# Modulation weights of a diffusion layer: 32 blocks over eight groups of tokens, all dot products on VectorE

## The chip, the cores and the metric

The kernel runs on one core of a Trainium2 chip. The metric is the device time of one execution, in microseconds. Five engines work beside each other, each with its own queue that is carried out in order: TensorE (PE; its weight loads are listed as PEld), VectorE (DVE), ScalarE (ACT), GpSimd (POOL) and SyncE (SP), which here issues all DMA transfers. Engines wait for each other by semaphores.

## The reference

One layer of a diffusion model in float32: 2048 latent tokens and 128 context tokens, width 1024. The part at issue comes first:

```python
def modulation(cond, w_ada, b_ada):
    m = jax.nn.silu(cond) @ w_ada + b_ada
    return jnp.split(m, 6, axis=-1)      # shift, scale, gate for attention and for the FFN

sa, ca, ga, sf, cf, gf = modulation(...)          # once for c, once for c_ctx
u = rms_norm(x, g_pre) * (1.0 + scale) + shift
p = u @ w_in                                       # q, k, v, B, C, x_in
```

`w_ada` is 1024 by 6144. It is used with two conditioning vectors, one for the latent and one for the context tokens. Then come differential attention (q and k of the latent tokens are rotated, softmax over 2176 keys), a gated short convolution, the output projection, and a SwiGLU FFN. Shift and scale of the attention (2048 columns) are needed before the first projection. The other 4096 columns (shift and scale of the FFN, both gates) are needed only after attention.

## The kernel before, in words

`w_ada` is stored transposed, in 48 blocks of 128 output columns (on partitions) by 1024 inputs, 512 KB each. For a block and a condition vector `ada_sum` makes 128 dot products of length 1024. On DVE (V) that is one instruction, line 139, which multiplies `raw` by the condition `cb` and sums into a column of `mc` (the full products go to `jv` and are not used). On POOL (G) it is a product, line 143 (`prod`), and a sum on ACT, line 144. The first 16 blocks are handled by `ada_first` before and during the first group of tokens; they are as they were.

Blocks 16 to 47 are handled by `ada_later`: one load (`raw`, four buffers), the dot product with the first vector on DVE, and that with the second on POOL for two blocks of three and on DVE for the third, as the string `LATER` says. So 32 + 11 products are on DVE and 21 on POOL. Small DVE instructions then turn the columns into `modc` (lines 149 to 151) or `gates` (line 174).

Phase 1 makes q, k and v in nine groups of tokens: eight of 256 latent tokens and one of the 128 context tokens, in the order 0, 1, 2, 8, 3, 4, 5, 6, 7 (8 is the context). Per group, `qkv_group` goes through k, q, v: 24 matmuls for each 128 tokens (lines 238 to 240, accumulator `pq`, four buffers). DVE reads `pq` for the rotation (line 291 and twice line 297, tile `t`), POOL adds the two parts (line 299), ACT and DVE split the sum into a high and a low part (`st`; lines 82 and 83), PE transposes it (line 250), ACT or DVE copies it out (`sto`, lines 254 and 256), and it is stored. Beside it, the next group is prepared: its rows are loaded (`xt`), scaled by POOL (line 203), transposed by PE (line 222, `up`), scaled and shifted by DVE (line 224, `ut`) and split (`uh`, `ul`).

After k, q and v of each group a step (`rows_step`, then `part_step` twice) prepares the next group and takes the next `PER` = 2 blocks from `ada_work`. So blocks 16 to 47 fall on the first six groups of the order: six to a group, two to the sixth. After the seventh (n == 6) the pools of the blocks and of the condition vectors are closed, and their room goes to phase 2.

The order on each engine is not the program's order: a scheduler with a model of the engines sets it when the kernel is built. Each instruction takes its place by when the model has it ready, so a product can stand before or after the group in which it is written. SP's queue has the loads of blocks, rows and weights, and all stores, in one order.

Phase 2 (attention, the convolution and the projection), the FFN and the end follow.

Of the kernel before, what the change touches and what calls it, by code (L numbers as in the profile page):

```python
# [32 lines left out]

POOLW = 960
WLV = (2,)
LATER = "GGV"
RAWS, PER, FIRST = 6, 2, "VG"
RATE = (670, 1500)


# [1 line left out]
def layer(ctx, tc, x_prompt, x_sample, cache_k, cache_v, cond, w_ada, b_ada, gcol,  # L42
# [3 lines left out]
    V, S, G, T = nc.vector, nc.scalar, nc.gpsimd, nc.tensor  # L46
# [24 lines left out]
    def dma(out, in_):  # L71

        out, in_ = (x.bitcast(F32) if x.dtype == F32R else x for x in (out, in_))
        with tc.issue_after(behind[0]) if behind else ExitStack():
            return nc.sync.dma_start(out, in_).ins
# [54 lines left out]
    def ada_load(b):  # L130
        raw = ad.tile([P, D], F32, tag="raw", name="raw", bufs=RAWS if b < 16 else 4)
        first[b] = dma(raw, w_ada[b])
        return raw

    def ada_sum(b, raw, c, eng):

        if eng is V:
            junk = cbp.tile([P, D], BF16, tag="jv", name="jv")
            V.scalar_tensor_tensor(junk, raw, 1.0, cb[:, c, :], op0=ALU.mult, op1=ALU.mult,
                                   accum_out=mc[:, b, c:c + 1])  # L140
        else:
            prod = cbp.tile([P, D], F32, tag="prod", name="prod", bufs=1)
            G.tensor_tensor(prod, raw, cb[:, c, :], op=ALU.mult)
            S.activation(prod, prod, AF.Copy, accum_out=mc[:, b, c:c + 1])

    def ada_cols(i, kt, cs):

        b = 8 * i + 2 * kt
        V.tensor_scalar(modc[:, i + 1, cs, kt], mc[:, b, cs], bc[:, b:b + 1], None, op0=ALU.add)
        V.tensor_scalar(modc[:, i, cs, kt], mc[:, b + 1, cs], bc[:, b + 1:b + 2], 1.0, op0=ALU.add, op1=ALU.add)  # L150
        V.tensor_scalar(modc[:, i, cs, kt], modc[:, i, cs, kt], gc[:, i // 2, kt:kt + 1], None, op0=ALU.mult)
# [13 lines left out]
    def ada_later(b):  # L165
        raw = ada_load(b)
        ada_sum(b, raw, 0, V)
        ada_sum(b, raw, 1, V if LATER[b % len(LATER)] == "V" else G)
        if b < 32:
            if b % 2:  # L170
                ada_cols(2, (b - 16) // 2, slice(0, 2))
            return
        which, k = divmod(b - 32, KT)
        V.tensor_scalar(gates[:, which, :, k], mc[:, b, :], bc[:, b:b + 1], gc[:, 2 + which, k:k + 1],
                        op0=ALU.add, op1=ALU.mult)
        if b == 47:
            ps = psu.tile([P, 512], F32, tag="psu", name="gt")
            T.transpose(ps[:32, :P], gates.rearrange("p w c k -> p (w c k)"), ident)
            gt = p1.tile([32, P], F32, name="gt")
            S.copy(gt, ps[:32, :P])  # L180
            dma(ggd.rearrange("w (k n) -> (w k) n", n=P), gt)
# [24 lines left out]
    def group_rows(gi):  # L206
        if gi == 8:
            return [norm_rows(x_prompt)]
        return [norm_rows(x_sample[(2 * gi + i) * P:(2 * gi + i + 1) * P, :]) for i in range(2)]

    def u_part(xs, gi, kk, between=None):

        n, c = len(xs), int(gi == 8)
        w = n * P
        up = psu.tile([P, 512], F32, tag="psu", name="up")
        ut = p1.tile([P, 2, 256], F32, tag="ut", name="ut", bufs=2)
        h = p1.tile([P, 2, 256], F32R, tag="uh", name="uh", bufs=6)
        l = p1.tile([P, 2, 256], F32R, tag="ul", name="ul", bufs=6)
        for a in range(2):
            kt = 2 * kk + a  # L220
            for i in range(n):
                T.transpose(up[:, a * 256 + i * P:a * 256 + (i + 1) * P],
                            xs[i][:, kt * P:(kt + 1) * P], ident)
            V.tensor_scalar(ut[:, a, :w], up[:, a * 256:a * 256 + w],
                            modc[:, 0, c, kt:kt + 1], modc[:, 1, c, kt:kt + 1],
                            op0=ALU.mult, op1=ALU.add)
            if between:
                split(h[:, a, :w], l[:, a, :w], ut[:, a, :w])
                between(kt, h[:, a, :], l[:, a, :])
        if not between:  # L230
            split(h[:, :, :w], l[:, :, :w], ut[:, :, :w])
        dma(ud[gi][0, :, 2 * kk:2 * kk + 2, :w], h[:, :, :w])
        dma(ud[gi][1, :, 2 * kk:2 * kk + 2, :w], l[:, :, :w])
        return [(h[:, a, :], l[:, a, :]) for a in range(2)]
# [127 lines left out]
    def qkv_group(gi, mid):  # L362

        n = 1 if gi == 8 else 2
        rt = None
        if gi < 8:
            rt = p1.tile([P, 2, 2, 64], F32, tag="rt", name="rt", bufs=2)
            dma(rt, rope[gi])
        for j in (1, 0, 2):
            sts = []  # L370
            for i in range(n):
                if gi == 0 and j < 2:
                    pq = pq0[i, j]
                else:
                    pq = psq.tile([P, 512], F32, tag="psq", name="pq")
                    for kt in range(KT):
                        qkv_mm(pq, u[gi], i, j, kt)
                qkv_out(pq, gi, i, j, rt, sts)
            mid[j]()
            out_stack(gi, j, sts)  # L380
            if j == 1 and "k" in mid:
                mid["k"]()

    def cached():
        ck = p1b.tile([P, 512], F32, tag="t1", name="ck", bufs=2)
        dma(ck, cache_k)
        stack([heads_split(ck)], k_store(NLAT), 0)
        cv = p1b.tile([P, 512], F32, tag="t1", name="cv", bufs=2)
        dma(cv, cache_v)
        v_split(cv, 16)  # L390
# [46 lines left out]
    ada_work = list(range(16, 48))  # L437
    rows = {}
    for n, gi in enumerate(order):
        nxt = order[n + 1] if n < 8 else None  # L440

        def rows_step():
            if nxt is not None:
                rows[nxt] = group_rows(nxt)
            for b in ada_work[:PER]:
                ada_later(b)
            del ada_work[:PER]

        def part_step(a):
            if nxt is not None:  # L450
                u.setdefault(nxt, [])
                for kk in (0, 1) if a == 0 else (2, 3):
                    u[nxt] += u_part(rows[nxt], nxt, kk)
            for b in ada_work[:PER]:
                ada_later(b)
            del ada_work[:PER]

        steps = {1: rows_step, 0: lambda: part_step(0), 2: lambda: part_step(1)}
        if nxt is None:
            steps["k"] = heads_begin  # L460
        qkv_group(gi, steps)
        behind.clear()
        if n == 0:
            cached()
        if n == 6:
            x_ad.close()
            x_cb.close()
    for x in (x_psq, x_psk, x_psu, x_pb, x_p1, x_wq):
# [211 lines left out]
    def t4(name):  # L680
        return prow.tile([P, D], F32, tag="t4", name=name, bufs=4)
# [385 lines left out]
    for gn, (c, g) in enumerate(groups):  # L1067
# [3 lines left out]
        for f in range(NF):  # L1071
            raw = t4("rawo")
# [85 lines left out]
```

## Time and profile before

| | us |
|---|---|
| median of three runs | 3112.84 |
| lowest, highest | 3108.48, 3118.28 |
| the profiled execution | 3102.96 |
| its span, from the first to the last instruction | 3101.2 |
| first score product of phase 2 (line 502) | 432.7 |

Times in the profile are counted from the span's start. Phase 1 is the first 430 us of it, a seventh. A busy share there is no measure of the whole span, so stretches of phase 1 are shown by themselves. Names in the rows are those of the program's tiles, without buffer numbers. An instruction's time includes what it waits once it has started; "idle before" is the time its engine had nothing to do just before it.

### The profile page before, as it was taken

Reading aid. Unit: us, or ns where it says so; the run is one execution under the profiler, and the core shown is the slowest. Engines: PE = TensorE matmul, PEld = TensorE weight load, DVE = VectorE, ACT = ScalarE, POOL = GpSimd, SP = SyncE. Lnnn points to the kernel's source line nnn. Section 1 sums busy time; section 2 is a strip of 40 time slices with the busy share of each in tenths; the row PEclk is TensorE's granted clock in tenths of the full one; section 3 lists DMA queues with packets and bytes.
Section 4 is the critical chain, followed back from the end, with each engine's and each line's share of the span. In section 5 each row is a group of like instructions: output and inputs, shape, how many; then the busy total and the mean of one; then the engine's idle time right before and its main releaser. Section 6 shows DMA issues by size and latency. Waiting matters only on the chain.

```text
span 3101.2 us, 47350 instructions
## 1 busy us (share of the span) xinstructions
PE 2926.7 (94%) x16921; PEld 2661.2 (86%) x16921; DVE 2080.6 (67%) x4116; ACT 1370.9 (44%) x2425; POOL 1296.4 (42%) x1135
## 2 busy tenths in 40 slices
PE   4789989999999999999999999999999999999998
PEld 3567879999999999988888888999899998788886
DVE  7996547887887887764467775676655554554443
ACT  3433225665655665663444343333333333443333
POOL 7653115554554554542246554554544540111110
PEclk8899999999999999999999999999999999999999
DMA  6776473463464354347635565434643235666663
GB/s 248 234 227 218 154 244 112 120 213 107 120 191 125 109 177 129 110 152 228 203 129 161 154 192 192 155 129 147 216 156 101 96 103 187 237 227 217 219 217 121
DMA packets 351180, 525.26 MB, mean 169 GB/s; under 512 B 33088, under 2 KB 264672, under 8 KB 349152
## 3 DMA queue, kind: packets, MB, share of 16 engines
q1 hardware_dynamic: 350944, 522.23, 52.7%
q8 instruction: 133, 2.18, 0.3%
q14 instruction: 103, 0.84, 0.1%
HBM read 393.79 MB, written 128.34 MB: 168 GB/s over the span
## 4 chain that ended last, share of the span: by engine, by line
PE 65%; DVE 14%; DMA 8%; issue 7%; POOL 4%; ACT 2%; SPq 0%; POOLq 0%; DVEq 0%; ACTq 0%
PE psg L956 7%; PE psg L959 6%; PE psg L957 6%; PE s L502 6%; PE psy L1087 4%; PE psy L1085 4%; PE psy L1086 4%; PE t L546 3%; DVE wi L83 2%; DMA raw<-in_w_fi 2%; PE psx L725 2%; PE psx L726 2%; PE psx L724 2%; PE o L539 2%; DMA u2d<-hl 2%
## 5 line engine op out<-in xcount | busy, mean ns | idle before, releaser
L956 PE MATMUL psg<-u,wi 128*128 128x384 f32 (+1 forms) x1848 | 617.4, 335 | 42.6 <-ACT wi L82 18.0
L957 PE MATMUL psg<-u,wi 128*128 128x384 f32 (+1 forms) x1848 | 607.3, 329 | 0.0
L959 PE MATMUL psg<-u,wi 128*128 128x384 f32 (+1 forms) x1848 | 591.5, 331 | 4.5 <-DVE wi L83 4.5
L505 DVE TENSOR_SCALAR_CACHE_REDUCE e<-s 128x436 f32<-128x436 f32 (+2 forms) x648 | 373.4, 600 | 87.0 <-PE s L502 71.4
L956 PEld LDWEIGHTS psg<-u,wi 128*128 128x128 f32 x1848 | 351.6, 190 | 61.7 <-ACT wi L82 27.6
L959 PEld LDWEIGHTS psg<-u,wi 128*128 128x128 f32 x1848 | 348.5, 190 | 9.0 <-DVE wi L83 8.5
L502 PE MATMUL s<-km,qt 128*128 128x436 f32 (+1 forms) x1280 | 344.4, 372 | 10.8 <-DVE e L505 8.5
L957 PEld LDWEIGHTS psg<-u,wi 128*128 128x128 f32 x1848 | 352.0, 190 | 0.1
L83 DVE TENSOR_TENSOR wo<-rawo,wo 128x1024 fp32r<-128x1024 f32 x132 | 167.0, 1265 | 248.6 <-ACT wo L82 243.9
L83 DVE TENSOR_TENSOR wi<-st,wi 128x512 fp32r<-128x512 f32 x264 | 234.4, 892 | 131.3 <-ACT wi L82 129.7
L510 ACT ACTIVATE e<-e,nm 128x2176 f32<-128x2176 f32 (+1 forms) x136 | 273.9, 2014 | 76.9 <-DVE nm L509 76.2
L82 ACT CAST wi<-st 128x512 fp32r<-128x512 f32 x264 | 163.0, 620 | 324.1 <-POOL st L918 161.4
L1087 PE MATMUL psy<-wo,hhl 128*128 128x512 f32 x748 | 285.5, 390 | 1.8 <-DVE hhl L83 1.8
L1086 PE MATMUL psy<-wo,hhl 128*128 128x512 f32 x748 | 285.9, 390 | 0.9 <-DVE wo L83 0.9
L1085 PE MATMUL psy<-wo,hhl 128*128 128x512 f32 x748 | 285.6, 390 | 0.0
L82 ACT CAST wo<-rawo 128x1024 fp32r<-128x1024 f32 x132 | 139.1, 1054 | 297.7 <-PE psy L1087 288.6
L502 PEld LDWEIGHTS s<-km,qt 128*128 128x128 f32 x1280 | 209.4, 190 | 23.6 <-DVE e L505 16.3
L83 DVE TENSOR_TENSOR atl<-t,ath 128x512 fp32r<-128x512 f32 (+2 forms) x292 | 187.2, 650 | 34.2 <-ACT ath L82 33.6
L82 ACT CAST ath<-t 128x512 fp32r<-128x512 f32 (+2 forms) x292 | 157.3, 555 | 113.6 <-PE t L546 111.1
L1058 POOL TENSOR_TENSOR rr<-rr,mhalf 128x1 f32<-128x1 f32 x17 | 13.1, 779 | 450.2 <-DVE rr L1057 450.2
L918 POOL TENSOR_TENSOR st<-raw,st 128x512 f32<-128x512 f32 x66 | 103.4, 1566 | 229.7 <-DVE wi L83 229.7
L238 PE MATMUL pq<-wh,uh 128*128 128x512 f32 x408 | 172.4, 433 | 19.9 <-DVE t L297 15.2
(264 smaller groups left out, 7183.9 us busy)
## 6 DMA issues: line engine op xcount, KB each, us to landing
raw<-in_w_fi SPq DMA_DIRECT2D x132, 512.0 KB, 4.1
rawo<-in_w_fo SPq DMA_DIRECT2D x132, 512.0 KB, 3.5
fu<-ud SPq DMA_DIRECT2D x256, 256.0 KB, 4.7
raw<-in_w_ada SPq DMA_DIRECT2D x48, 512.0 KB, 4.8
u2d<-hl SPq DMA_DIRECT2D x42, 512.0 KB, 3.8
u<-u2d SPq DMA_DIRECT2D x14, 1536.0 KB, 9.5
hr<-hid SPq DMA_DIRECT2D x110, 192.0 KB, 3.5
hid<-hid SPq DMA_DIRECT2D x88, 192.0 KB, 1.9
```

The lines of the kernel that those rows point to most:

```text
L82: S.copy(h, src)
L83: (eng or V).tensor_tensor(l, src, h.bitcast(F32), op=ALU.subtract)
L238: T.matmul(pq, u[kt][0][:, sl], wh[j, kt], start=(kt == 0), stop=False)
L502: mm = T.matmul(ps[:, :n], qt[:, s, m, t * P:(t + 1) * P], km[m][:, k0:k0 + n], start=(s == 0), stop=(s == 1))
L505: V.tensor_scalar(et[:, k0:k0 + n], ps[:, :n], SCALE, None, op0=ALU.mult, op1=ALU.max, accum_out=mx[:, ci:ci + 1])
L510: S.activation(et[:, :nk], et[:, :nk], AF.Exp, bias=nm, scale=1.0, accum_out=sm[:, t, m:m + 1])
L956: T.matmul(ps[:, :n], h[:, ks], u[:, 0, kt, :n], start=start and kt == 0, stop=False, skip_group_check=not start)
L957: T.matmul(ps[:, :n], h[:, ks], u[:, 1, kt, :n], start=False, stop=False, skip_group_check=not start)
L959: T.matmul(ps[:, :n], l[:, ks], u[:, 0, kt, :n], start=False, stop=stop and kt == 3, skip_group_check=not start)
L1085: T.matmul(banks[i][:, b, :], hh, woh_[:, bs], start=(f == 0), stop=False)
L1086: T.matmul(banks[i][:, b, :], hh, wol_[:, bs], start=False, stop=False)
L1087: T.matmul(banks[i][:, b, :], hl, woh_[:, bs], start=False, stop=(f == NF - 1))
```

## The change: what it does

All second dot products of blocks 16 to 47 are on DVE as well: 64 on DVE and none on POOL. Per group of the order, four blocks are taken (two in `rows_step`, one in each `part_step`) instead of six, so the 32 blocks fall on eight groups. The pools are closed one group later. `ada_first` still puts one product of each pair on POOL.

```diff
-LATER = "GGV"
-RAWS, PER, FIRST = 6, 2, "VG"
+RAWS, FIRST = 6, "VG"
...
     def ada_later(b):
         raw = ada_load(b)
         ada_sum(b, raw, 0, V)
-        ada_sum(b, raw, 1, V if LATER[b % len(LATER)] == "V" else G)
+        ada_sum(b, raw, 1, V)
...
+        def ada_steps(k):
+            for b in ada_work[:k]:
+                ada_later(b)
+            del ada_work[:k]
+
         def rows_step():
             if nxt is not None:
                 rows[nxt] = group_rows(nxt)
-            for b in ada_work[:PER]:
-                ada_later(b)
-            del ada_work[:PER]
+            ada_steps(2)
...
-            for b in ada_work[:PER]:
-                ada_later(b)
-            del ada_work[:PER]
+            ada_steps(1)
...
-        if n == 6:
+        if n == 7:
             x_ad.close()
             x_cb.close()
```

By the order, the sequences of all engines are the same up to early in group 0's outputs and from phase 2 on; between them instructions change places. On DVE, 67 dot products become 88. Between the first of the 32 rotations (line 291) and the thirteenth, that of group 3's first 128 tokens, 43 products and 16 `gates` stood; now 47 and 7 do. Line numbers of the new kernel are lower by one in this part.

DVE before, around the first rotation of group 3 (`jv` is a dot product, `t_2011<-pq` the rotation's first part, `bl` a weight split for phase 2):

```order
L139 SCALAR_TENSOR_TENSOR jv,mc<-raw,cb 128x1024
L256 CAST sto<-tp 128x2x128
L83 TENSOR_TENSOR ul<-ut,uh 128x512
L224 TENSOR_SCALAR ut<-up,modc 128x256
L174 TENSOR_SCALAR gates<-mc,bc,gc 128x2
L91 TENSOR_SCALAR rr<-ss 128x1
L224 TENSOR_SCALAR ut<-up,modc 128x256
L91 TENSOR_SCALAR rr<-ss 128x1
L256 CAST sto<-tp 128x2x128
L83 TENSOR_TENSOR bl<-braw,bh 128x512
L291 TENSOR_TENSOR t_2011<-pq,rt 128x512
L297 TENSOR_TENSOR t_2012<-pq,rt 128x16x16 x2
```

The same place now (`t_1939` is the same rotation):

```order
L173 TENSOR_SCALAR gates<-mc,bc,gc 128x2
L138 SCALAR_TENSOR_TENSOR jv,mc<-raw,cb 128x1024 x2
L173 TENSOR_SCALAR gates<-mc,bc,gc 128x2
L138 SCALAR_TENSOR_TENSOR jv,mc<-raw,cb 128x1024
L290 TENSOR_TENSOR t_1939<-pq,rt 128x512
L296 TENSOR_TENSOR t_1940<-pq,rt 128x16x16 x2
L90 TENSOR_SCALAR rr<-ss 128x1
L290 TENSOR_TENSOR t_1973<-pq,rt 128x512
L138 SCALAR_TENSOR_TENSOR jv,mc<-raw,cb 128x1024
L223 TENSOR_SCALAR ut<-up,modc 128x256 x2
L296 TENSOR_TENSOR t_1974<-pq,rt 128x16x16 x2
L173 TENSOR_SCALAR gates<-mc,bc,gc 128x2
```

Before, the last product stood ahead of that rotation, and phase 2's weight splits had begun; now products stand right ahead of it and between the two parts of the next rotation, and go on through groups 3 and 4.

POOL before, from group 2 to group 8's rows (`t` is the rotation's sum, `prod` a product, `rr` and `xt` belong to the next group's rows):

```order
L299 TENSOR_TENSOR t_1379<-t_1379,t_1380 128x512
L143 TENSOR_TENSOR prod<-raw,cb 128x1024 x2
L299 TENSOR_TENSOR t_1413<-t_1413,t_1414 128x512
L143 TENSOR_TENSOR prod<-raw,cb 128x1024
L299 TENSOR_TENSOR t_1504<-t_1504,t_1505 128x512
L143 TENSOR_TENSOR prod<-raw,cb 128x1024 x2
L299 TENSOR_TENSOR t_1538<-t_1538,t_1539 128x512
L143 TENSOR_TENSOR prod<-raw,cb 128x1024 x2
L92 TENSOR_TENSOR rr<-rr,mhalf 128x1
L203 TENSOR_SCALAR xt<-xt,rr 128x1024
```

The same place now:

```order
L298 TENSOR_TENSOR t_1341<-t_1341,t_1342 128x512
L298 TENSOR_TENSOR t_1375<-t_1375,t_1376 128x512
L298 TENSOR_TENSOR t_1465<-t_1465,t_1466 128x512
L298 TENSOR_TENSOR t_1499<-t_1499,t_1500 128x512
L91 TENSOR_TENSOR rr<-rr,mhalf 128x1
L202 TENSOR_SCALAR xt<-xt,rr 128x1024
```

The products are gone, and the rotation's sums and the rows' instructions follow each other.

## Rows read from the trace of the kernel before

**Rows 1.** The page: the span, and each engine's busy time over it.

```profile
span 3101.2 us, 47350 instructions
PE 2926.7 (94%) x16921; PEld 2661.2 (86%) x16921; DVE 2080.6 (67%) x4116; ACT 1370.9 (44%) x2425; POOL 1296.4 (42%) x1135
```

**Rows 2.** Stretches: busy us and instructions by engine, granted clock, DMA share, GB/s.

```profile
core 0: us, PE busy (x) PEld busy (x) DVE busy (x) ACT busy (x) POOL busy (x), PEclk, DMA share, GB/s
107.00:245.00 138.00, 112.23 (x502) 87.24 (x501) 137.89 (x213) 49.60 (x92) 88.09 (x39) 0.90 0.72 234
...
290.00:410.00 120.00, 120.00 (x601) 98.05 (x600) 58.54 (x110) 27.85 (x51) 24.87 (x21) 1.00 0.53 171
```

**Rows 3.** Waits of PE, 107 to 245 us: us in total, times, longest.

```profile
PE pq L238 <- DVE t L297: 15.2, 5, 7.0
PE tp L250 <- ACT sto L254: 4.7, 2, 3.7
PE tp L250 <- DVE sto L256: 4.3, 4, 2.6
```

**Rows 4.** Waits of PE, 245 to 410 us.

```profile
PE pq L238 <- ACT uh L82: 0.4, 1, 0.4
```

**Rows 5.** DVE's groups by shape, 107 to 262 us: busy us, mean ns, idle before.

```profile
L139 DVE SCALAR_TENSOR_TENSOR jv<-raw,cb 128x1024 bf16<-128x1024 f32 x43 | 64.7, 1504 | 0.0
L151 DVE TENSOR_SCALAR modc<-modc,gc 128x2 f32<-128x2 f32 x8 | 11.1, 1388 | 0.0
L83 DVE TENSOR_TENSOR st<-t,st 128x512 fp32r<-128x512 f32 x11 | 10.4, 952 | 0.0
L149 DVE TENSOR_SCALAR modc<-mc,bc 128x2 f32<-128x2 f32 x8 | 9.0, 1123 | 0.0
L297 DVE TENSOR_TENSOR t<-pq,rt 128x256 f32<-128x256 f32 x22 | 8.2, 411 | 0.0
...
L83 DVE TENSOR_TENSOR ul<-ut,uh 128x512 fp32r<-128x512 f32 x7 | 7.4, 1058 | 0.0
...
L83 DVE TENSOR_TENSOR ul<-ut,uh 128x256 fp32r<-128x256 f32 x4 | 5.4, 1366 | 0.0
L150 DVE TENSOR_SCALAR modc<-mc,bc 128x2 f32<-128x2 f32 x8 | 4.1, 510 | 0.0
```

**Rows 6.** All dot products on DVE: ns min/median/max, first and last start.

```profile
L139 DVE SCALAR_TENSOR_TENSOR jv<-raw,cb x67: 1208/1215/3411, 8.0 to 251.8; 128x1024 bf16<-128x1024 f32 x67
```

**Rows 7.** One of the small instructions on `modc`, likewise.

```profile
L151 DVE TENSOR_SCALAR modc<-modc,gc x24: 195/209/2355, 10.9 to 191.2; 128x1 f32<-128x1 f32 x16, 128x2 f32<-128x2 f32 x8
```

**Rows 8.** DVE in order of time, 147 to 154 us: start, us, instruction.

```profile
149.83 3.41 DVE L139 SCALAR_TENSOR_TENSOR jv<-raw,cb 128x1024 bf16<-128x1024 f32 x1
```

**Rows 9.** POOL in order of time, the same stretch.

```profile
149.26 2.89 POOL L143 TENSOR_TENSOR prod<-raw,cb 128x1024 f32<-128x1024 f32 x1
```

**Rows 10.** POOL's groups by shape, 107 to 262 us.

```profile
L143 POOL TENSOR_TENSOR prod<-raw,cb 128x1024 f32<-128x1024 f32 x21 | 58.2, 2771 | 37.2 <-DMA raw<-in_w_ada 30.7 <-ACT prod L144 5.3 <-DMA qd<-sto 1.3
L299 POOL TENSOR_TENSOR t<-t,t 128x512 f32<-128x512 f32 x12 | 22.4, 1867 | 9.6 <-DVE t L297 9.6
```

**Rows 11.** DVE's groups by shape, 290 to 410 us.

```profile
L83 DVE TENSOR_TENSOR st<-t,st 128x512 fp32r<-128x512 f32 x12 | 10.0, 837 | 3.7 <-ACT st L82 3.7
...
L83 DVE TENSOR_TENSOR ul<-ut,uh 128x512 fp32r<-128x512 f32 x12 | 7.8, 688 | 1.5 <-ACT uh L82 1.4
```

**Rows 12.** DVE in order of time, 133 to 139 us.

```profile
135.41 1.21 DVE L139 SCALAR_TENSOR_TENSOR jv<-raw,cb 128x1024 bf16<-128x1024 f32 x1
...
136.55 0.22 DVE L149 TENSOR_SCALAR modc<-mc,bc 128x2 f32<-128x2 f32 x1
```

**Rows 13.** The stretch of groups 3 and 4, columns as in rows 2.

```profile
260.00:335.00 75.00, 74.64 (x378) 60.83 (x377) 41.12 (x81) 23.37 (x43) 20.16 (x15) 1.00 0.62 200
```

**Rows 14.** POOL's rotation sums: ns min/median/max, first and last start.

```profile
L299 POOL TENSOR_TENSOR t<-t,t x32: 1264/1601/3422, 100.4 to 419.1; 128x512 f32<-128x512 f32 x32
```

**Rows 15.** Phase 2's score products, likewise.

```profile
L502 PE MATMUL s<-km,qt x1280: 352/361/732, 432.7 to 1354.1; 128*128 128x436 f32 x147, 128*128 128x432 f32 x36
```

## The prediction

> **What bounds the kernel now.** I first read the page's totals [rows 1]: over the whole span TensorE (PE) is the busy engine, and VectorE (DVE) has a third of the time free. That average hides the stage the change touches, so next came the table by stretches [rows 2]. From 107 to 245 us DVE is busy for 137.89 of 138 us, PE runs 502 instructions, and its granted clock averages 0.90. From 290 to 410 us, where the same group code runs without modulation blocks, DVE is busy 58.54 of 120 us, PE runs 601 instructions without a gap, and its granted clock is 1.00. At that later rate, 120 / 601 = 0.200 us per instruction, the 502 instructions need 100.2 us. The stretch therefore loses 137.9 - 100.2 = 37.7 us, partly in gaps and partly in matmuls at the lower of the two levels (1.2 and 2.4 GHz) behind each gap. That is the most this change can return there.
>
> Third, PE's waits. The three longest kinds in that stretch are on DVE's rotation, on ACT's copy and on DVE's copy, 15.2 + 4.7 + 4.3 = 24.2 us [rows 3]; from 245 to 410 us one wait of 0.4 us is left [rows 4]. So PE is the bound after 245 us, and DVE's in-order queue is the bound before it.
>
> Fourth, why DVE is full. The groups of one shape [rows 5] show means far over what the same shapes take undisturbed. A dot product has a mean of 1504 ns against a median of 1215 [rows 6]; the three small instructions on the `modc` columns have means of 1388, 1123 and 510 ns, where the shortest takes 195 [rows 7]; `st` takes 952 and the large `ul` 1058, against some 680 of `ul` in the quiet stretch [rows 11]. The rotation's halves, which read PSUM, take 411 ns here too; the small `ul` of the same 256 columns takes 1366. One product shows the cause: it starts at 149.83 and lasts 3.41 us, and a GpSimd (POOL) product that started at 149.26 runs for 2.89 us, to 152.15 [rows 8, 9]. From there to the DVE product's end are 1.1 us, one free product. DVE stood until POOL was done.
>
> The Trainium skill says the same of such pairs ("SBUF — State Buffer", section "Who interferes with whom"): a DVE instruction with two SBUF inputs, or in a two-port mode, and a GpSimd instruction that reads SBUF exclude each other for a whole instruction. By that rule, the trace agrees: only the groups with SBUF sources are stretched.
>
> **The change part by part.**
> (a) *21 POOL products and 21 sums on ACT go.* ACT is not full, so its part counts zero. POOL's part counts through DVE. Waiting in the groups of rows 5, busy time less count times the free duration: products 64.7 - 43 x 1.215 = 12.5; `modc` 9.5 + 7.4 + 2.5; `st` 2.9 and `ul` 2.6 (free 0.68) and 3.8 (free 0.41). Together 41.2 us. What stays comes from POOL's rotation sums and row scalings. Upper bound: POOL is busy 88.1 us in the stretch and its products take 58.2 of them [rows 2, 10], so 29.9 / 88.1 of 41.2 = 14.0 us. Lower bound: the quiet stretch, where `st` loses 10.0 - 12 x 0.68 = 1.8 us and `ul` nothing [rows 11]. Those 1.8 us fall on 24 instructions; in the full stretch about 93 are exposed, which gives 7. I take 7, so DVE loses 34.2 us of waiting.
>
> (b) *21 more products on DVE, in another order.* Started back to back, one costs the step from 135.41 to 136.55, 1.14 us [rows 12]. All blocks have two products on DVE now, and each group gets four blocks instead of six, so a group still brings eight products. By the order, 47 products (was 43) stand before the first rotation of group 3, and 7 gate instructions (was 16); the other 17 products and 9 gates stand in groups 3 and 4. In the full stretch this adds 4 x 1.14 = 4.6 us and takes away 9 x 0.2 = 1.8. DVE's sum: 137.9 - 34.2 + 4.6 - 1.8 = 106.5 us. That is still a little over PE's 100.2, so DVE sets the end and 31.4 us are won, if DVE never stands idle.
>
> (c) *DVE's own idle time.* A full DVE has none (0.1 us). With 6 us between the two engines it will wait now and then, for a weight block above all, and everything queued behind a waiting product (rotation, `st`, `sto`, `ut`) waits with it, and PE for those. Lower end 0.1 us; upper end 30.7, what POOL waited for blocks in the same stretch [rows 10]. DVE comes late to its products, as it did before, so I stay nearer the lower end: 10 us.
>
> (d) *Groups 3 and 4.* From 260 to 335 us DVE is busy 41.1 of 75 us [rows 13]. It gains 17 x 1.14 + 9 x 0.2 = 21.2 us, perhaps 2 us of waiting, which makes 64 of 75 (less, since phase 2's first weight splits leave this stretch), and PE's continuous work hides it. Bounds: 0, and 8 us if PE waits for late instructions a third as long as in rows 3; I take 0.5.
>
> (e) *Queues.* The 32 block loads stay; each block's buffer is given back by DVE alone. The row loads of the next group stand a little later among them on SyncE's queue, behind stores. Full PE work in the quiet stretch hides such a load now; its price if uncovered is part of (c). Closing the two pools one group later moves phase 2's first weight splits to groups 4 and 5, still ahead of their first use in phase 2: nothing. The order is the same from phase 2 on, so what phase 1 wins the end wins.
>
> Sum: 31.4 - 10 - 0.5 = 21 us. Against the profiled execution's 3102.96 us (span 3101.2 plus 1.8 around it) that gives 3082. That execution lies 9.9 us below the runs' median of 3112.84, so for a median I subtract the same 21: 3092.
>
> **The rivals.**
> 1. *PE becomes the bound everywhere.* If DVE's idle times fall where PE is busy anyhow, the whole 37.7 us come back: 3075. For it: PE has four accumulators to run ahead in, and the gap between the engines is small. Against it: DVE's sum is still the longer.
> 2. *POOL comes late instead: no change.* The added products hold POOL out just as POOL held DVE. The row shows its rotation sums at 1867 ns in the stretch [rows 10], against 1264 for the shortest [rows 14], and `st`, the transposes and PE wait for these sums. A sum can lose up to one product, 1.21 us; 12 of them make 14.5 us, all on the path. Then 21 - 14.5 = 6.5 us are left: 3106, which a measurement of this kernel can't tell from no change (0.3%, 9.3 us). Against it: PE had no long wait for `st` in rows 3, and POOL has more room.
> By the Trainium skill's rule on the same page and section, the instruction issued first keeps the port; so which side loses is open, and either 21 or 6.5 would stand. The trace shows DVE losing in row 8 and the sums losing in row 10.
> 3. *DVE waits for the blocks: slower.* POOL waited 30.7 us for 21 blocks. If DVE, no longer late, meets each of the 32 first products that early, it waits 32 / 21 x 30.7 = 46.8 us, in order and with all else behind it. It decides from 31.4 us on; at its full price the time is 15 us longer: 3128. For it: POOL's nine waits, up to 6.9 us. Against it: POOL could run ahead to the block because it had little else in its queue, while DVE has a rotation or split between most products; and buffers come back sooner.
> 4. *The order doesn't spread them.* The program spreads 64 products over eight groups, the order still puts 47 before group 3. That is in (b) already; it is why I don't count a relief of DVE's own work.
>
> **How the numbers follow.** Chances: forecast 0.65 (10 to 31 us won: 3082 to 3103), rival 1 0.11, rival 2 or a similar stop 0.15, rival 3 0.09. Faster by over 0.3%: the forecast and rival 1, 0.76; within 0.3%: rival 2 and the mild half of rival 3, 0.17; slower: 0.07. Range for 8 in 10: from rival 1's 3075 up to 3110, which takes in rival 2 and leaves out rival 3.
>
> **What would show it.** In the changed profile, from 107 us on: products near 1.25 us in the mean and `modc` near 0.2; at most some 10 us of DVE idle, on blocks or rows; PE's instructions of 107 to 245 us done by about 225; phase 2's first score product, now at 432.7 us [rows 15], near 412. Wrong, if products on DVE wait over 30 us for their loads, if `modc` and products stay stretched without POOL's products, if PE waits over 20 us for `st` behind POOL's sums, or if PE has gaps in groups 3 and 4.

## The result, and the profile after

The changed kernel takes 3083.06 us in the median (3080.67 to 3085.89, four runs), against 3112.03 us before (3108.48 to 3118.28, four runs): a ratio of 0.9914, with a 95% interval of 0.9898 to 0.993, so 22 to 32 us faster. The forecast was 3092, with a range of 3075 to 3110.

First, where in the span the time went. The first line is the page's span, the second the score products of phase 2 (line 502; ns min/median/max, first and last start), both of the changed kernel:

```profile
span 3084.1 us, 47310 instructions
...
L502 PE MATMUL s<-km,qt x1280: 352/361/735, 408.0 to 1336.4; 128*128 128x436 f32 x147, 128*128 128x432 f32 x36
```

Against [rows 15], phase 2 begins 432.7 - 408.0 = 24.7 us earlier. The spans differ by only 17.1 us [rows 1]. The rest of the program, whose order is the same in both, took 2676.1 us here and 2668.5 in the profiled execution before, which was 9 us below the median of its kernel. In the twelve traces of this case that rest takes between 2668.5 and 2679.4 us, whether phase 1 is long or short. So the two traces tell what phase 1 won, and the repeated runs tell the total; 24.7 lies inside their interval.

Next, the same stretches as in [rows 2, 13]: busy time and instructions by engine, granted clock, DMA.

```profile
core 0: us, PE busy (x) PEld busy (x) DVE busy (x) ACT busy (x) POOL busy (x), PEclk, DMA share, GB/s
107.00:225.00 118.00, 109.72 (x531) 86.19 (x530) 110.74 (x215) 28.08 (x54) 27.86 (x17) 0.97 0.78 251
107.00:245.00 138.00, 129.72 (x627) 102.34 (x626) 129.19 (x252) 33.51 (x64) 37.55 (x23) 0.98 0.78 253
...
260.00:335.00 75.00, 75.00 (x389) 61.32 (x388) 60.13 (x110) 24.51 (x44) 22.94 (x16) 1.00 0.66 221
```

From 107 to 245 us PE now runs 627 instructions instead of 502, at a granted clock of 0.98 instead of 0.90; the 125 more are worth 25 us at 0.200 us each. DVE has free time again, 8.8 of 138 us. The largest of PE's waits between 107 and 225 us (total, times, longest):

```profile
PE tp L249 <- ACT sto L253: 3.8, 2, 2.0
PE up L221 <- DVE ut L223: 1.6, 3, 1.0
PE pq L237 <- DVE t L296: 1.4, 1, 1.4
PE tp L249 <- DVE st L82: 0.6, 1, 0.6
```

The wait for the rotation has fallen from 15.2 to 1.4 us [rows 3]. The longest that is left, 2.0 us up to 213.13, is for a copy by ACT that waited 2.30 us for a store (`ud<-uh`) to land; from 210 to 220 us the granted clock averages 0.66, and PE runs 24 instructions in these 10 us, where 50 would fit at 0.200 us each. DVE's groups of one shape from 107 to 248 us, to be held against [rows 5]:

```profile
L138 DVE SCALAR_TENSOR_TENSOR jv<-raw,cb 128x1024 bf16<-128x1024 f32 x50 | 64.6, 1291 | 0.1
L82 DVE TENSOR_TENSOR st<-t,st 128x512 fp32r<-128x512 f32 x13 | 10.7, 827 | 0.0
L296 DVE TENSOR_TENSOR t<-pq,rt 128x256 f32<-128x256 f32 x24 | 8.9, 407 | 0.0
...
L82 DVE TENSOR_TENSOR ul<-ut,uh 128x512 fp32r<-128x512 f32 x9 | 6.0, 680 | 0.0
L148 DVE TENSOR_SCALAR modc<-mc,bc 128x2 f32<-128x2 f32 x8 | 4.8, 594 | 0.0
...
L150 DVE TENSOR_SCALAR modc<-modc,gc 128x2 f32<-128x2 f32 x8 | 3.5, 443 | 0.0
...
L82 DVE TENSOR_TENSOR ul<-ut,uh 128x256 fp32r<-128x256 f32 x4 | 2.8, 689 | 0.0
```

Fifty products take the busy time that 43 took (64.6 and 64.7 us). The groups shown that read SBUF have come down, and the rotation's halves, which read PSUM, have hardly moved (411 and 407 ns).

### The profile page after: what moved, and what is told of

It reads as the page before. It is cut to its first block, busy times and chain, and to the rows that moved or that the text cites. A ratio compares the mean times of both kernels' runs of the same rounds, so it can differ in the third digit from the quotient of the medians.

```text
span 3084.1 us, 47310 instructions
## 1 busy us (share of the span) xinstructions
PE 2914.8 (95%) x16921; PEld 2653.6 (86%) x16921; DVE 2082.6 (68%) x4158; ACT 1348.7 (44%) x2383; POOL 1242.9 (40%) x1114
## 4 chain that ended last, share of the span: by engine, by line
PE 65%; DVE 12%; DMA 9%; issue 7%; POOL 4%; ACT 2%; SPq 1%; POOLq 0%; DVEq 0%; ACTq 0%
PE psg L956 6%; PE s L502 6%; PE psg L959 6%; PE psg L957 6%; PE psy L1087 4%; PE psy L1086 4%; PE psy L1085 4%; PE t L546 3%; DVE wi L82 3%; DMA raw<-in_w_fi 2%; PE pq L239 2%; POOL st L918 2%; PE psx L725 2%; PE psx L726 2%; PE psx L724 2%
## 5 line engine op out<-in xcount | busy, mean ns | idle before, releaser
L82 DVE TENSOR_TENSOR wi<-raw,wi 128x512 fp32r<-128x512 f32 x198 | 176.6, 892 | 15.7 <-ACT wi L81 15.7
```

The source lines that it names most:

```text
L82: (eng or V).tensor_tensor(l, src, h.bitcast(F32), op=ALU.subtract)
```

## The experiments

The theory: POOL's products blocked DVE through SBUF, and their removal is the whole gain. The main rivals: the spreading over eight groups relieves DVE; or DVE was simply full of its own work. Ratios are against the kernel before, whose runs lay around 3111 us.

**Only the products** (six blocks a group as before):

```diff
-LATER = "GGV"
+LATER = "V"
```

> Only the first part of the change: all second products of blocks 16 to 47 on DVE, six blocks a group as before. Port theory (POOL's products made DVE wait; taking them away is the whole gain): as the changed kernel, 3083, first score product at 405 to 412 us. Rival (the spreading over eight groups relieves DVE): without it DVE has 12 products a group in the first five groups, 4 x 1.14 = 4.6 us more in each, so 15 to 23 us of the 29 are lost: 3098 to 3106.

Measured: 3084.99 us, ratio 0.9917 (0.9904 to 0.9931), phase 2 from 409.9 us. That is the whole gain, as near as the runs can tell (3083.06 with both parts). By the order, 47 products stand before group 3's first rotation in this kernel too.

**Only the spreading** (the changed program with `LATER = "GGV"` kept):

```diff
         def rows_step():
...
-            for b in ada_work[:PER]:
+            ada_steps(2)
...
-        if n == 6:
+        if n == 7:
```

> Only the other part: four blocks a group over eight groups, the second products two of three on POOL as before. Port theory: POOL's 21 products stay, the scheduler puts them where they were, so as before, 3108 to 3114, and DVE full with products of some 1.5 us in the mean. Rival (spreading): 15 to 23 us faster, 3090 to 3097.

Measured: 3110.51 us, ratio 1.0001 (0.999 to 1.0013): nothing. From 107 to 245 us in this kernel, the stretch and the dot products on DVE:

```profile
107.00:245.00 138.00, 109.92 (x488) 85.33 (x487) 137.89 (x213) 49.37 (x92) 87.29 (x39) 0.88 0.72 234
```

```profile
L139 DVE SCALAR_TENSOR_TENSOR jv<-raw,cb 128x1024 bf16<-128x1024 f32 x39 | 58.7, 1505 | 0.0
```

DVE is full for the same 137.89 us as in [rows 2], with products as long as in [rows 5]. DVE's order in phase 1 is that of the kernel before but for two instructions that stand a few places off: in whatever group the blocks are written, the scheduler put their products in the same places.

**All second products on POOL:**

```diff
-LATER = "GGV"
+LATER = "G"
```

> The kernel before with all 32 second products on POOL (DVE has 11 fewer). Port theory: 11 more POOL products at the same share of waiting (34 us for 21, so 18 us) against 11 x 1.14 = 12.5 us less work on DVE: 0 to 10 us slower than before, 3111 to 3121. Rival (DVE was full of its own work): 12 us faster, 3099.

Measured: 3114.99 us, ratio 1.0007 (0.9998 to 1.0016). Taking 11 products off the full engine gained nothing. The stretch from 107 to 245 us, the dot products on DVE in it, and the products on POOL up to 262 us:

```profile
107.00:245.00 138.00, 111.09 (x501) 86.66 (x500) 130.70 (x186) 53.60 (x100) 97.10 (x43) 0.91 0.69 217
```

```profile
L139 DVE SCALAR_TENSOR_TENSOR jv<-raw,cb 128x1024 bf16<-128x1024 f32 x26 | 45.6, 1755 | 3.3 <-DMA raw<-in_w_ada 3.3
```

```profile
L143 POOL TENSOR_TENSOR prod<-raw,cb 128x1024 f32<-128x1024 f32 x29 | 81.0, 2792 | 22.8 <-ACT prod L144 20.9 <-DMA raw<-in_w_ada 1.9
```

The 26 products that are left on DVE take 1755 ns in the mean; the 39 of the same stretch before took 1534. DVE is busy for 130.70 of 138 us, so part of the work that it lost came back as waiting and part became idle time. PE runs 501 instructions, as before (502): it got nothing of either. That speaks against DVE's own work as the cause.

**POOL's products left out** (the context's column is then a copy of the latent one's, so this part is not computed):

```diff
-        ada_sum(b, raw, 1, V if LATER[b % len(LATER)] == "V" else G)
+        if LATER[b % len(LATER)] == "V":
+            ada_sum(b, raw, 1, V)
+        else:
+            V.tensor_copy(mc[:, b, 1:2], mc[:, b, 0:1])
```

> The kernel before with the 21 POOL products and their sums on ACT left out; a copy of the other column stands in for them, so the modulation of the context tokens is not the reference's. DVE's own products stay as they were (43 in groups). Port theory: all of PE's loss in the stretch comes back, 25 to 37 us: 3075 to 3086, no more than 8 us under the changed kernel, DVE busy about 100 of 138 us from 107 us on. Rival (DVE's own work): DVE has as much to do as before, no change, 3111.

Measured: 3083.41 us, ratio 0.9907 (0.9892 to 0.9922), DVE busy 127.97 of 138 us (not the 100 expected: the same 138 us now hold more of the order, 641 PE instructions instead of 502). Two readings follow. Without POOL's products the gain is there although DVE has as many products as before. And the changed kernel, which puts the 21 on DVE, is no slower in the median (3083.06): their 21 x 1.14 = 24 us of DVE's time cost little. In the traces phase 2 begins at 402.7 us here and at 408.0 in the changed kernel, so phase 1 may pay some 5 us for them; the totals don't show it. This run leaves out ACT's 21 sums too; the next one keeps them.

**What of a POOL instruction stops DVE?** The 21 products are replaced by fills that read nothing (their results are not computed; ACT's sums, now line 148, stay):

```diff
-            G.tensor_tensor(prod, raw, cb[:, c, :], op=ALU.mult)
+            if b < 16:
+                G.tensor_tensor(prod, raw, cb[:, c, :], op=ALU.mult)
+            else:
+                for _ in range(3):
+                    G.memset(prod, 0.0)
```

> The kernel before, with each of POOL's 21 products of blocks 16 to 47 replaced by three fills of the same tile, which read nothing (the second column of these blocks is then zero, not the reference's). It asks what of a POOL instruction stops DVE. If it is POOL's reading (the rule of the Trainium skill, SBUF - State Buffer, Who interferes with whom, for a DVE instruction with two SBUF inputs), DVE's products of 107 to 245 us fall from 1.50 to at most 1.32 us as in the kernel with the products left out, and `modc`, one input in a two-port mode, may stay stretched (0.4 to 1.3 us): 3080 to 3095. If any busy POOL stops DVE, products stay near 1.5 us: 3105 to 3115.

Measured: 3080.91 us, ratio 0.9899 (0.9884 to 0.9913). From 107 to 245 us POOL is busy 89.00 us, as long as before. First two groups of DVE, then one of POOL, in that stretch:

```profile
L139 DVE SCALAR_TENSOR_TENSOR jv<-raw,cb 128x1024 bf16<-128x1024 f32 x43 | 52.2, 1214 | 0.0
...
L155 DVE TENSOR_SCALAR modc<-modc,gc 128x2 f32<-128x2 f32 x8 | 6.8, 848 | 0.0
```

```profile
L147 POOL MEMSET prod<- 128x1024 f32 x51 | 48.7, 954 | 17.8 <-ACT prod L148 16.3
```

With POOL just as busy, DVE's products take their free 1.21 us: the longest of the 43 takes 1.23, though 26 of them run beside a fill. So what stops them is not a busy POOL but POOL's reading of SBUF, and since ACT's sums are still there, the gain doesn't come from leaving those out. The small `modc` instructions stay at 848 ns against some 200 free. Twelve of the 24 take over 0.3 us, and each of the twelve ends 0.02 to 0.03 us after a fill ends. One place shows both, on DVE and then on POOL (start, us, instruction):

```profile
116.13 0.45 DVE L153 TENSOR_SCALAR modc<-mc,bc 128x2 f32<-128x2 f32 x1
...
116.32 1.21 DVE L139 SCALAR_TENSOR_TENSOR jv<-raw,cb 128x1024 bf16<-128x1024 f32 x1
```

```profile
115.60 0.95 POOL L147 MEMSET prod<- 128x1024 f32 x1
```

The fill ends at 116.55 us and `modc` at 116.58; the product starts during the fill and takes no longer than a free one. By the Trainium skill ("SBUF — State Buffer", section "Who interferes with whom"), a DVE instruction with two SBUF inputs contends with a GpSimd instruction that reads SBUF and not with one that only writes it, and one in a two-port mode contends with GpSimd. The trace agrees on the first with 1214 ns. On the second it shows fills holding `modc`; that `modc` runs in such a mode is not shown by itself.

**The same step in group 0:** the last eight products on POOL go to DVE.

```diff
-RAWS, FIRST = 6, "VG"
+RAWS, FIRST = 6, "VV"
```

> The changed kernel with the same step in group 0: the eight second products of blocks 0 to 15 that are still on POOL go to DVE too. In the changed kernel DVE is full from 20 to 70 us and its 24 products there take 1.95 us in the mean, 17.6 us of waiting in all. Port theory: 8 x 1.14 = 9 us are added, some 10 to 15 us of waiting go: 1 to 8 us faster than the changed kernel, 3075 to 3082. Rival (DVE's own work or the loads bound group 0): 0 to 9 us slower, 3083 to 3092.

Measured: 3069.61 us, ratio 0.9863 (0.9848 to 0.9879): 13 us under the changed kernel, beyond the range expected, and faster than both kernels. From 20 to 80 us, the products on DVE in the changed kernel, and then in this one:

```profile
L138 DVE SCALAR_TENSOR_TENSOR jv<-raw,cb 128x1024 bf16<-128x1024 f32 x20 | 41.9, 2095 | 0.0
```

```profile
L138 DVE SCALAR_TENSOR_TENSOR jv<-raw,cb 128x1024 bf16<-128x1024 f32 x26 | 42.8, 1645 | 0.0
```

Six more products for 0.9 us of DVE's time. Phase 2 begins at 399.4 us, 8.6 us earlier than in the changed kernel; the other part of the 13 us is not in phase 1 of this trace.

**Also the weight splits of group 0 on DVE:**

```diff
-WLV = (2,)
+WLV = (0, 1, 2)
-RAWS, FIRST = 6, "VG"
+RAWS, FIRST = 6, "VV"
```

> As the one with the first products on DVE, and the 16 splits of the q and k weights move from POOL to DVE: POOL is left with the rows and the rotation's sums. Port theory: 16 x 0.6 = 9.6 us more on DVE, its remaining waits in group 0 go: 0 to 8 us faster than the changed kernel, 3075 to 3083. Rival (DVE's own work): 10 to 19 us slower, 3093 to 3102.

Measured: 3070.59 us, ratio 0.9865 (0.9849 to 0.9882). Products come down to 1296 ns from 20 to 80 us and `ul` to its free 414, which pays for 16 splits on DVE; the total is as in the run before, neither better nor worse. Like that run it lies under the range expected (3075 to 3083), which was counted from the changed kernel.

**The rotation's sums on DVE:**

```diff
-        G.tensor_tensor(t1, t1, t2, op=ALU.add)
+        V.tensor_tensor(t1, t1, t2, op=ALU.add)
```

> The changed kernel with the rotation's 32 sums on DVE instead of POOL: 32 x 0.6 = 19 us more work on DVE, 1.9 us less a sum on POOL, and most of the 13 us of waiting that DVE still has from 107 to 245 us goes. If what is left of that waiting still sets the end: 3 to 8 us faster, 3075 to 3080. If PE is the bound there now (the kernel with the products left out was no faster than the changed one): 0 to 5 us either way, 3079 to 3088.

Measured: 3078.43 us, ratio 0.9893 (0.9878 to 0.9908). `st` falls to 683 ns and products to 1222; phase 2 begins at 400.4 us. The median lies in the first range, but the interval (3074 to 3083) reaches into the second, so the total does not tell the two apart. The trace does in part: phase 2 begins 7.6 us earlier than in the changed kernel, so PE was not yet the bound of all of phase 1 there.

**Both**, first products and sums on DVE:

> Both gains together: first products on DVE (13 us under the changed kernel) and the rotation's sums on DVE (5 us under it). Port theory: they lie in different stretches (20 to 107 us, and after 107 us), so they add: 3062 to 3067. Rival (DVE becomes the bound again with 29 more instructions' work after 107 us and PE is already full there): no more than the first products alone, 3069 or above.

Measured: 3073.74 us, ratio 0.9881 (0.9864 to 0.9897). The two gains don't add, as the rival said, but not for its reason: from 107 to 245 us DVE is busy for 126.24 of 138 us, so it is not the bound again. Waits of PE from 107 to 410 us:

```profile
PE tp L249 <- ACT sto L253: 7.7, 5, 3.5
PE s L502 <- DVE sto L255: 3.4, 1, 3.4
PE up L221 <- DVE ut L223: 0.9, 1, 0.9
```

PE waits for ACT's copies instead (1.0 us with the first products alone); phase 2 begins at 400.4 us, no earlier than with either part.

**And the scaling of the rows on ACT:**

```diff
-        G.tensor_scalar(xt, xt, r, 1.0, op0=ALU.mult, op1=ALU.mult)
+        S.activation(xt, xt, AF.Copy, scale=r)
```

> As before it, and the scaling of the rows on ACT: POOL has almost nothing left in phase 1 but the 16 weight splits of group 0. Port theory: the first two scalings (xt waits of PE, 18.9 us before 107 us) and the last waits of DVE change by a few us: 3058 to 3066. Rival (PE's own work is the bound, and ACT's copies `sto` come later): as the one with two gains or up to 5 us slower, 3064 to 3071.

Measured: 3064.35 us, ratio 0.984 (0.9825 to 0.9855), the fastest median of all. It is clear of the run with both (0.9864 to 0.9897) and overlaps the first products alone (0.9848 to 0.9879) by a little. The median lies in both ranges expected, so the total does not choose between them. Of the reasons given, PE's wait for the first rows hardly changed: 17.1 us before 107 us, 19.6 in the run with both. Phase 2 begins 10.7 us earlier than in that run:

```profile
L502 PE MATMUL s<-km,qt x1280: 352/361/713, 389.7 to 1315.6; 128*128 128x436 f32 x147, 128*128 128x432 f32 x36
```

POOL is busy 6.26 us from 107 to 245 us, and PE runs 678 instructions there, at a granted clock of 1.00. Which of the moves gave how much stays open.

## Why the prediction was right, point by point

*What bounds.* Right: most of the loss of 37.7 us from 107 to 245 us was DVE's, and DVE's was POOL's. Of the three runs that could have said otherwise, none did: spreading alone 1.0001, fewer products on DVE 1.0007, no products on POOL 0.9907. The prediction showed one product that stood behind POOL. In that trace, nine of the 43 products from 107 to 262 us take over 1.3 us, and each of the nine ends 1.08 to 1.09 us after a POOL instruction ends: six after a `prod`, three after a rotation sum. Their extra time is 12.5 us, all the waiting that the prediction counted for products. Of the 24 `modc`, 14 take over 0.3 us, and each ends 0.02 to 0.03 us after a POOL instruction.

*(a) The waiting that stays.* Taken as 7 us, bounds 1.8 and 14.0. In the changed kernel, by the same working over the groups shown up to 248 us and the third `modc` group (2.1 us): products 64.6 - 50 x 1.215 = 3.9, `modc` 3.2 + 1.9 + 0.5, `st` 1.9, `ul` 1.2, together 12.6 us. So the term was too small, and `modc` did not come down to near 0.2 us as foreseen (594, 267 and 443 ns). What it was said to come from is right: in the changed kernel's trace the seven products of 107 to 262 us that take over 1.3 us end behind five rotation sums and two row scalings, and with the sums on DVE the products come down to 1222 ns. The scaling from the quiet stretch was too low, probably because DVE has half its time free there and seldom starts something while POOL is at work; the other bound, by POOL's busy time, was the nearer one.

*(b) DVE's sum.* The counts up to group 3's first rotation held (47 and 7). But that rotation starts at 260.5 us before and 237.0 now, not where the stretch ends: PE's 502nd instruction from 107 us on ends at 245.2 us before and 219.4 now. Up to there DVE did 39 products and 12 `gates` before, 41 and 4 now, so the added work was two products and not four. The changed kernel up to that point:

```profile
107.00:219.40 112.40, 104.12 (x503) 81.73 (x502) 108.85 (x212) 27.15 (x51) 27.86 (x17) 0.97 0.79 253
```

DVE's busy time, foreseen as 106.5 us, was 108.85; the waiting that was taken too small (10.4 us up to there by the working of (a), not 7) and the added work that was taken too large (0.7 us, not 2.8) partly cancel, which is luck.

*(c) DVE's idle time.* Taken as 10 us; 112.40 - 108.85 = 3.5 us up to 219.4, and 7.3 us up to 225. This is the term that was most wrong. DVE's three largest waits up to 225 us:

```profile
DVE ut L223 <- PE up L221: 3.7, 1, 3.7
DVE rr L90 <- ACT junk L200: 1.3, 1, 1.3
DVE sto L255 <- DMA kd<-sto: 0.7, 1, 0.7
```

No wait for a weight block is among them or the smaller ones. So rival 3 fell. The reason given against it, that POOL had met the blocks early because it had little else to do, fits the run with all second products on POOL: there POOL waited 1.9 us for blocks instead of 30.7. That was not tested further.

*(d) Groups 3 and 4.* Foreseen as 64 of 75 us of DVE, or somewhat less, and no loss on PE: 60.13, and PE busy for 75.00. From 225 to 410 us PE has one wait left, 2.2 us for a copy by ACT.

*Sum.* The stretch was to end 106.5 + 10 = 116.5 us after 107 and ended after 112.4. DVE was busy for nearly all of that, as foreseen, with less idle time. That its work and waiting still set most of the length is also what the run with the rotation's sums on DVE says: there the same instruction of PE ends at 212.9 us. From 219.4 us to phase 2 the changed kernel takes 188.6 us, the one before 187.5 from its 245.2. So phase 1 was to win 21 us, with phase 2 from 412 us, and won 24.7, from 408.0.

*Rival 1.* Not the whole 37.7 us came back: 245.2 - 219.4 = 25.8. PE still waits 8.2 us from 107 to 225 us, and with more work taken off POOL, phase 2 begins as early as 389.7 us.

*Rival 2.* Its mechanism is in the trace, its price is not. POOL's rotation sums from 107 to 248 us:

```profile
L298 POOL TENSOR_TENSOR t<-t,t 128x512 f32<-128x512 f32 x12 | 23.1, 1925 | 51.9 <-DVE modc L149 26.3 <-DVE t L296 23.0 <-DVE modc L150 2.6
```

They are as long as before (1867 ns, [rows 10]). Eight of the twelve take over 2 us; each of the eight starts while a DVE product runs and ends 1.14 to 1.16 us after it, where the shortest sum takes 1.26. One of them, with the product that it stands behind:

```profile
171.90 1.21 DVE L138 SCALAR_TENSOR_TENSOR jv<-raw,cb 128x1024 bf16<-128x1024 f32 x1
```

```profile
172.12 2.13 POOL L298 TENSOR_TENSOR t<-t,t 128x512 f32<-128x512 f32 x1 [5.05 <-DVE t L296]
```

So DVE's products do hold the sums up, by some 0.66 us a sum in the mean (1925 less 1264) and not by the 1.21 taken as the most. But PE waits only 0.6 us behind `st` for its transposes. That the sums have PE's next passes as cover is the likely reason; no run tests it.

*Rival 4.* It said that the order doesn't spread the products; the run with spreading alone shows no effect of this part of the change (0.999 to 1.0013).

*Open.* The medians differ by 29 us and phase 1's ends in the two traces by 24.7; whether the other 4 us are more than the spread between executions can't be told from one profile each. Why PE got nothing from DVE's idle time with all second products on POOL is not worked out either.

## What to carry to other kernels

A busy DVE may be a waiting DVE: compare each shape's mean with its shortest or its mean in a quiet stretch, and if only the shapes that read SBUF are stretched, see whether the long ones end a fixed time after a POOL instruction. Here products with two SBUF inputs stood only behind POOL instructions that read SBUF; the small `modc` stood behind fills too. Work that moves from POOL to DVE can then be free, or better: moving 21 products of 1.14 us to the full engine made phase 1 faster by 24.7 us. When a scheduler sets the order, look there before crediting a loop's new shape with anything.

## What was not expected of the hardware

POOL filling SBUF for 48.7 us left DVE's two-input products at their free 1214 ns, while it held the small `modc` until the fill's end; for the products, reading was what counted. A dot product of 1024 elements with its sum takes 1.14 us from start to start [rows 12], and a `tensor_tensor` of 512 about 0.60 us (`st` in the same view, from 136.75 to 137.34 us), so the sum costs next to nothing per element.
